# One product of 512 columns and one of 256 per weight block, a bank per output tile, and w_down behind w_up

## The chip, the cores and the metric

The kernel runs on one core of a Trainium2 chip. Times are device microseconds of one execution, from a profiler or from repeated timed runs; the number compared is the median of the timed runs. PE is the matrix engine, PEld its weight loads, DVE the vector engine, ACT the scalar engine, POOL the general engine, SP the engine whose queue issues the DMAs.

## The reference

Two blocks run one after the other on 256 positions of 1024 features. The change lies in the first block, in its output projection and its feed-forward part:

```python
x = x + jnp.einsum("bsd,de->bse", g_a * y_a + g_b * y_b, w_o[i])

h = rmsnorm(x, g_ffn[i])
u = jnp.einsum("bsd,df->bsf", h, w_up[i])                       # 1024 -> 2 * 2816
f_gate = causal_dwconv(u[..., :D_FF], conv_f_w[i]) + conv_f_b[i]   # 3 taps
f = jax.nn.gelu(f_gate, approximate=True) * u[..., D_FF:]
x = x + jnp.einsum("bsf,fd->bsd", f, w_down[i])                 # 2816 -> 1024

pg = jax.nn.sigmoid(jnp.einsum("bsd,de->bse", rmsnorm(x, g_ple[i]), w_ple_gate[i]))
x = x + pg * jnp.einsum("bsk,kd->bsd", p[i], w_ple[i])
...
```

Ahead of it stand a gated convolution mixer (w_in, w_a_out, w_b_out), behind it a final norm and a second block with windowed and differential attention and a feed-forward part of its own (w_up_2, w_down_2). All of it is float32.

## The kernel before

**Data.** Activations lie with features on the 128 partitions and the 256 positions along the free axis, so a tile of 128 features is 128x256. Weights come from memory in groups of eight blocks of 128x128 (`GROUPS`, 128x1024, 512 KB), in the order in which `_order` lists them; the names raw58, hi58 and lo58 carry the number of the group.

**Two parts.** Each float32 operand is split into a high part in the matrix engine's reduced format and the remainder. For a weight group, ACT casts raw into hi (`split_task`) and DVE subtracts to make lo; for an activation tile likewise, into two tiles called cr. A product of a weight block and an activation tile is three matrix products, which `run` issues: wh by xh, wh by xl, wl by xh, each of 256 columns, all three added up in one half of a PSUM bank (`Bank.half`). A bank (ps) holds two output tiles. Six hi and six lo buffers exist, and a split is begun four groups ahead of its use (`LEAD`).

**Order.** `Plan` is a small planner that runs when the program is built. It keeps a clock for every engine and writes each instruction into its engine's queue when the planner's clock says that its inputs are there; on the chip every queue runs in order, and waits are semaphores. Work around the products is written as generators (`f1_task`, `res_task`, `norm_task`) that the planner continues between matrix products (`plan.work`) or until a condition holds (`plan.until`).

**The stretch that is changed.** `w_o` has 8 x 8 weight blocks. When a pair of its output tiles is done, `res_task` adds x, makes the scaled split h2 of the new x, and squares it into a sum kept by POOL (`Sum`). `norm_task` takes the sum: a product with a column of 1/1024 (the tile is called mean in the profile and mean1024 in the program), an addition on DVE, a power of -0.5 on POOL (small), a product that spreads the two columns over the partitions (ident and small), and a copy by ACT into r2. `w_up` starts before r2 is there, on h2, which lacks that factor; `evac_pair` multiplies it in when a bank is taken out of PSUM. `w_up` has 22 pairs of tiles (gate j and value 22 + j), 16 blocks each. `f1_task` then does the convolution (one ACT instruction and two on DVE), the GELU, the product with the value tile and the split into `f[j]`. After pair j, `w_down` takes the eight blocks of row j - 4 (`LAG1`), adding to eight output tiles that keep four banks for the whole stretch. After the last row, `res_task` runs for all eight tiles, the sum and norm for r3 follow, and `w_ple_gate` goes on with h3.

Of the kernel before, what the change touches and what calls it, by code (L numbers as in the profile page):

```python
# [17 lines left out]
P = 128  # L18
# [25 lines left out]
LAG1, LAG2 = 4, 6  # L44
# [6 lines left out]
def _order():  # L51
# [17 lines left out]
    def ffn(up, down, n, lag, first, whole):  # L69
# [8 lines left out]
    ffn("w_up", "w_down", 22, LAG1, 2, False)  # L78
# [11 lines left out]
    ffn("w_up_2", "w_down_2", 32, LAG2, 4, True)  # L90
# [61 lines left out]

class Plan:
# [11 lines left out]
    def at(self, tiles):  # L165
        return max([self.written.get(t.tensor.name, 0.0) for t in tiles], default=0.0)

    def op(self, eng, cost, outs, ins, port=False):

        names = [t.tensor.name for t in outs]  # L170
# [15 lines left out]
        for t in ins:  # L186
            self.read[t.tensor.name] = max(self.read.get(t.tensor.name, 0.0), end)
# [133 lines left out]
def block_kernel(ctx: ExitStack, tc: tile.TileContext, w, xT, pT, vec, dist, gpost, out):  # L321
# [41 lines left out]
    NC = 79  # L363
# [4 lines left out]
    def cr():  # L368
        return ap.tile([P, T], F32R, tag="c", name=nm("cr"), bufs=NC)

    def pair():
        return ap.tile([P, 2, T], F32, tag="pair", name=nm("pair"), bufs=10)
# [76 lines left out]
    def run(key, dst, xs, lastk, hook=None):  # L449

        for n, b in enumerate(ORDER[key]):
# [6 lines left out]
            xh, xl = xs[k]  # L458
            plan.work(plan.at((wh, wl, xh, xl)))
# [5 lines left out]


    vt = cpool.tile([P, NV], F32, name="vt")
    gm = cpool.tile([P, 8], F32, name="gm")
    x = [cf() for _ in range(8)]
# [140 lines left out]
    def xn_task():  # L610
# [109 lines left out]
    def gate_task(c, q):  # L720
        yield [q.t]
        if c < 4:
            yield lambda: r1[0] is not None
            u = evac_pair(q, r1[0])
            yield [u]
        for i in range(2):
            g = cf()
            S.activation(g, u[:, i, :] if c < 4 else q.half(i), AF.Sigmoid, bias=vec1("b_gate", c + i))
            gates[c + i] = g
# [24 lines left out]
    def sc_task(c, q, qb):  # L754
# [12 lines left out]
        hi, lo = cr(), cr()  # L767
        S.copy(hi, qb.half(0))
        yield [hi]
        V.tensor_tensor(lo, qb.half(0), hi.bitcast(F32), op=ALU.subtract)  # L770
        shl[c] = hi, lo
# [37 lines left out]
    def yb_task(j, q):  # L809
        yield [q.t]  # L810
        for i in range(2):
            t = cf()
            V.tensor_tensor(t, q.half(i), gates[8 + j + i], op=ALU.mult)
            yb[j + i] = t
# [10 lines left out]
    def yp_task(j, q):  # L825
        yield [q.t]
        for i in range(2):
            t = cf()
            S.copy(t, q.half(i))
            yp[j + i] = t  # L830
# [17 lines left out]
    def mix_task(j, q):  # L848
        yield [q.t]
        for i in range(2):  # L850
            t = cf()
            V.tensor_tensor(t, q.half(i), gates[j + i], op=ALU.mult)
            V.tensor_tensor(t, t, yb[j + i], op=ALU.add)
            plan.spawn(split_task2(t, mix, j + i))
# [9 lines left out]
    def res_task(j, q, s, h, g):  # L864

        yield [q.t]
        for i in range(2):
            t = cf()
            V.tensor_tensor(t, q.half(i), x[j + i], op=ALU.add)
            x[j + i] = t  # L870
            hi = cr()
            S.activation(hi, t, AF.Identity, scale=vec1(g, j + i))
            plan.spawn(lo_scaled(t, hi, vec1(g, j + i), h, j + i, s))

    plan.spawn(norm_task(s2, DM, r2))
    qs = [Bank(), Bank()]
    run(("w_o", 0), {m: (qs[m // 2], m % 2) for m in range(4)}, mix, 7)
    plan.spawn(res_task(0, qs[0], s2, h2, "g_ffn"))
    plan.spawn(res_task(2, qs[1], s2, h2, "g_ffn"))
    del qs  # L880
    for j in (4, 6):
        q = Bank()
        run(("w_o", j), {j: (q, 0), j + 1: (q, 1)}, mix, 7)
        plan.spawn(res_task(j, q, s2, h2, "g_ffn"))
# [12 lines left out]
    def f1_task(j, q):  # L897
# [13 lines left out]
        V.tensor_tensor(c, c, u[:, 1, :], op=ALU.mult)  # L911
        ups[1] += 1
        yield [c]
        hi, lo = cr(), cr()
        S.copy(hi, c)
        yield [hi]
        V.tensor_tensor(lo, c, hi.bitcast(F32), op=ALU.subtract)
        f[j] = hi, lo

    ffn_first("w_up", 2, 22, h2, f1_task)  # L920
    down = [Bank() for _ in range(4)]
    ddst = {m: (down[m // 2], m % 2) for m in range(8)}
    for j in range(2, 22):
        plan.until(lambda: ups[0] > j - 4)
# [11 lines left out]
    for j in range(0, 8, 2):  # L936
        plan.spawn(res_task(j, down[j // 2], s3, h3, "g_ple"))
    del down, ddst
# [18 lines left out]
    def ple_task(j, q):  # L957
# [4 lines left out]
        ts = []  # L962
        for i in range(2):
            t = cf()
            S.activation(t, u[:, i, :], AF.Sigmoid)
            ts.append(t)
        if j == 6:
            preload(AF.Exp)
        hs = []
        for i in range(2):  # L970
# [5 lines left out]
            hi = cr()  # L976
            S.activation(hi, t, AF.Identity, scale=gfp[:, j + i : j + i + 1])
            hs.append(hi)
        for i in range(2):
            yield [hs[i]]  # L980
            lo = cr()
            V.scalar_tensor_tensor(
                lo, ts[i], gfp[:, j + i : j + i + 1], hs[i].bitcast(F32), op0=ALU.mult, op1=ALU.subtract
            )
            h4[j + i] = hs[i], lo
# [26 lines left out]
    def r45_task():  # L1012
# [23 lines left out]
        for j in range(8):  # L1036
            yield "dve"
            t = cf()
# [7 lines left out]
    def sc_tile(tag, bufs):  # L1046
        return ap.tile([P, 3 * P], F32, tag=tag, name=nm(tag), bufs=bufs)
# [86 lines left out]
    def swa_task():  # L1134
# [6 lines left out]
        for g in range(2):  # L1141
            pts = []
            for b in range(3):
# [4 lines left out]
                t = ap.tile([P, 512], F32, tag="pT", name=nm("pT"), bufs=4)  # L1148
# [16 lines left out]
        for b in range(2):  # L1165
            yield [yo[b].t]
            sq = ap.tile([P, 512], F32, tag="pT", name=nm("pT"), bufs=4)
# [17 lines left out]
        for c in range(4):  # L1185
# [7 lines left out]
            hi, lo = cr(), cr()  # L1193
            S.copy(hi, t)
            yield [hi]
            V.tensor_tensor(lo, t, hi.bitcast(F32), op=ALU.subtract)
            mix[c] = hi, lo
# [4 lines left out]
    for k in range(8):  # L1202
# [3 lines left out]
        plan.work(plan.at((wh, wl) + h4[k]))  # L1206
        for tt in range(2):
            plan.work()
            xh, xl = (z[:, tt * P : (tt + 1) * P] for z in h4[k])
# [38 lines left out]
    def diff_task(h, q):  # L1248
# [51 lines left out]
        hi, lo = cr(), cr()  # L1300
        S.copy(hi, y)
        yield [hi]
        V.tensor_tensor(lo, y, hi.bitcast(F32), op=ALU.subtract)
        mix[4 + h] = hi, lo
# [21 lines left out]
    for p in range(4):  # L1326
        sq = ap.tile([P, 512], F32, tag="pT", name=nm("pT"), bufs=4)
# [21 lines left out]
    def x5_task():  # L1349
        for j in range(8):  # L1350
            t = og[j // 2][:, j % 2, :]
            V.tensor_tensor(t, t, q6[:, T:], op=ALU.mult)
            n = cf()
            V.tensor_tensor(n, t, x[j], op=ALU.add)
            x[j] = n
            hi = cr()
# [183 lines left out]
```

## Time and profile before

| | before |
|---|---|
| median of 3 timed runs | 783.16 us (782.24 to 783.36) |
| the profiled execution's own time | 782.5 us |
| its span, first to last instruction | 780.7 us |
| PE busy | 762.9 us, 98% of the span |
| DVE busy | 613.3 us, 79% |
| ACT busy | 439.1 us, 56% |
| POOL busy | 95.1 us, 12% |
| granted PE clock, mean | 0.997 |

The span lies inside the execution's own time; 1.8 us are around it. Busy time of PE is modelled from pipelined products, so it tells that products are in flight, not that they could not follow each other faster. What a product costs is read from the distance between starts of neighbouring products.

### The profile page before, as it was taken

The page shows a single profiled execution, that of the slowest core. Times are in us where ns is not written, and L with a number is a line of the kernel's source. Part 1 is how long each engine was busy: PE and PEld are TensorE (multiplying, and loading weights), DVE is VectorE, ACT ScalarE, POOL GpSimd, SP SyncE. Part 2 cuts the span into 40 slices and gives each one's busy share as a digit, 9 for nine tenths or more (in the row PEclk, how much of TensorE's full clock was granted, in tenths as well). Part 3 has the DMA queues.
Part 4 walks back from the last instruction along what each step waited for, and adds up shares of the span by engine and source line. Part 5 has one row for each costly group of instructions (what it writes and reads, how often), then busy time and mean ns, then how long its engine had stood idle before and what let it go on. Part 6 is the DMA issues. An engine that isn't in the chain of part 4 may idle for free.

```text
span 780.7 us, 14974 instructions
## 1 busy us (share of the span) xinstructions
PE 762.9 (98%) x5892; PEld 735.2 (94%) x5892; DVE 613.3 (79%) x1099; ACT 439.1 (56%) x757; POOL 95.1 (12%) x75
## 2 busy tenths in 40 slices
PE   7999999999999999999999999999999999999996
PEld 6999999999999999999999799899999999999995
DVE  5699978877766676678679797789987877878783
ACT  6566465565544544456648655657755555554551
POOL 1589200040000000003200001220000000000000
PEclk9999999999999999999999999999999999999998
DMA  8757647564556555655344344363755555555631
GB/s 290 232 181 220 194 130 239 169 188 157 173 194 200 168 176 187 200 167 170 107 130 149 123 153 144 108 209 106 235 181 195 183 189 190 189 182 177 203 114 54
DMA packets 39670, 135.75 MB, mean 174 GB/s; under 512 B 4528, under 2 KB 6320, under 8 KB 39600
## 3 DMA queue, kind: packets, MB, share of 16 engines
q1 hardware_dynamic: 39600, 134.80, 53.5%
q8 instruction: 46, 0.75, 0.4%
q14 instruction: 24, 0.20, 0.1%
HBM read 133.73 MB, written 1.05 MB: 173 GB/s over the span
## 4 chain that ended last, share of the span: by engine, by line
PE 90%; DVE 3%; POOL 2%; issue 2%; DMA 1%; ACT 1%; SPq 0%; DVEq 0%; POOLq 0%
PE ps L272 90%; DVE cf L272 2%; POOL cf L272 2%; DVE lo L272 1%; DMA raw<-w_in 1%; DMA cf<-xT_in 1%; POOL small L272 0%; SPq L272 0%; ACT hi L272 0%; DVE pair L272 0%; ACT pT L272 0%; DVE cr L272 0%; DVEq L1535 0%; ACT cf L272 0%; DVE ps L272 0%
## 5 line engine op out<-in xcount | busy, mean ns | idle before, releaser
L272 PE MATMUL ps<-cr,hi 128*128 128x256 f32 x3408 | 621.8, 285 | 5.4 <-ACT hi L272 5.1
L272 PEld LDWEIGHTS ps<-cr,hi 128*128 128x128 f32 x3408 | 534.0, 192 | 10.0 <-ACT hi L272 5.5
L272 PE MATMUL ps<-cr,lo 128*128 128x256 f32 x1704 | 483.0, 283 | 0.8 <-DVE lo L272 0.8
L272 PEld LDWEIGHTS ps<-cr,lo 128*128 128x128 f32 x1704 | 327.3, 192 | 1.2 <-DVE lo L272 1.2
L272 DVE TENSOR_TENSOR lo<-raw,hi 128x1024 fp32r<-128x1024 f32 (+2 forms) x237 | 285.0, 1215 | 44.2 <-ACT hi L272 43.1
L272 ACT CAST hi<-raw 128x1024 fp32r<-128x1024 f32 (+2 forms) x255 | 258.7, 1027 | 45.9 <-PE ps L272 26.6
L272 ACT ACTIVATE cf<-pair,vt 128x256 f32<-128x256 f32 x90 | 50.0, 594 | 97.8 <-DVE pair L272 97.8
L272 DVE SCALAR_TENSOR_TENSOR cf<-pair,vt,cf 128x255 f32<-128x255 f32 (+1 forms) x172 | 80.1, 482 | 30.5 <-ACT cf L272 27.3
L272 PE MATMUL ps<-hi,cr 128*128 128x512 f32 (+2 forms) x320 | 98.2, 375 | 0.0
L272 PEld LDWEIGHTS ps<-hi,cr 128*128 128x128 f32 x320 | 58.9, 188 | 10.5 <-issue 1.0
L272 POOL TENSOR_TENSOR cf<-cf,cf 128x256 f32<-128x256 f32 x28 | 34.4, 1228 | 273.5 <-DVE cr L272 186.4
L272 POOL TENSOR_TENSOR small<-small,mh 128x2 f32<-128x2 f32 (+1 forms) x15 | 15.3, 1023 | 396.9 <-DVE small L272 396.9
L272 ACT CAST cr<-cf 128x256 fp32r<-128x256 f32 x76 | 30.5, 405 | 55.8 <-DVE cf L272 55.5
L272 PE MATMUL ps<-lo,cr 128*128 128x512 f32 (+2 forms) x160 | 60.0, 375 | 0.0
L272 ACT ACTIVATE cf<-cf 128x256 f32<-128x256 f32 x102 | 39.3, 411 | 33.7 <-DVE cf L272 33.7
L272 DVE TENSOR_TENSOR pair<-ps,cf 128x512 f32<-128x512 f32 x60 | 41.0, 688 | 16.7 <-PE ps L272 12.3
L272 DVE SCALAR_TENSOR_TENSOR cf<-ps,vt,cf 128x255 f32<-128x255 f32 (+30 forms) x136 | 51.9, 453 | 0.3 <-ACT cf L272 0.2
L272 POOL TENSOR_TENSOR lo<-raw,hi 128x1024 fp32r<-128x1024 f32 x18 | 42.9, 2419 | 10.0 <-ACT hi L272 10.0
L272 DVE TENSOR_TENSOR cr<-cf,cr 128x256 fp32r<-128x256 f32 x74 | 30.7, 421 | 11.8 <-ACT cr L272 11.7
L272 PEld LDWEIGHTS ps<-lo,cr 128*128 128x128 f32 x160 | 30.2, 189 | 4.0
L272 DVE TENSOR_TENSOR cf<-cf,cf 128x256 f32<-128x256 f32 x64 | 26.4, 420 | 1.0
L272 ACT ACTIVATE cr<-cf,vt 128x256 fp32r<-128x256 f32 x24 | 11.0, 502 | 16.6 <-DVE cf L272 16.5
(102 smaller groups left out, 302.4 us busy)
## 6 DMA issues: line engine op xcount, KB each, us to landing
raw<-w_in SPq DMA_DIRECT2D x244, 512.0 KB, 4.0
raw<-w_in SPq DMA_DIRECT2D x8, 320.0 KB, 2.9
cf<-xT_in SPq DMA_DIRECT2D x8, 128.0 KB, 5.7
out<-pT SPq DMA_DIRECT2D x3, 256.0 KB, 2.0
pair<-gpost_in SPq DMA_DIRECT2D x2, 256.0 KB, 5.9
vt<-vec_in SPq DMA_DIRECT2D x1, 420.5 KB, 5.9
dt<-dist_in SPq DMA_DIRECT2D x1, 384.0 KB, 5.8
raw<-w_in SPq DMA_DIRECT2D x2, 128.0 KB, 2.3
```

What stands on the lines that cost most here:

```text
L272: r = f(*args, **kw)
```

## The change

**Products.** `run2` takes the place of `run` for w_o, for w_up from pair 4 on, and for w_down. The two parts of an activation tile now stand side by side in one tile of 128x2x256 (`parts`), and the product of wh with both is one product of 512 columns into a whole bank; wl by xh follows with 256 columns into the bank's first half. The result is the sum of the two halves, so each output tile has a bank of its own, and the task that reads the bank adds the halves.

**Tasks.** `res2_task` adds x to the second half and then the first half to that, two DVE additions for one. `f1b_task` takes the place of `f1_task` from pair 4 on: ACT copies the second half of the gate's bank out, DVE adds it to the first half in PSUM, the convolution reads PSUM; the same for the value, whose product and split are done in PSUM. There the factor r2 can't be applied on the way out, since the banks hold unscaled halves; so `normed_task` makes a second, normalised split hn2 of x (one DVE multiplication, one ACT cast, one DVE subtraction per tile) for pairs 4 to 21. Pairs 0 to 3 (`OLD1`) go on as before.

**Order.** All of w_up comes first, then w_down, tile by tile over all 22 rows, the first two output tiles together (`DOWN1`).

**Buffers.** 79 buffers of 128x256 and 10 pairs become 16 and 56; gates, yb, yp and x move into pairs.

```diff
+    o["w_up", 0] = _blocks("w_up", (0, 22, 1, 23), r8)
+    for j in range(2, 22):
+        o["w_up", j] = _blocks("w_up", (j,), r8) + _blocks("w_up", (22 + j,), r8)
+    o["w_down", 0] = _blocks("w_down", range(DOWN1), range(22))
+    for m in range(DOWN1, 8):
+        o["w_down", m] = _blocks("w_down", (m,), range(22))
...
+    def run2(key, dst, xs, lastk):
+        for _, k, m in ORDER[key]:
+            if xs[k] is None:
+                plan.until(lambda: xs[k] is not None)
+            wh, wl = block((key[0], k, m))
+            xp = xs[k]
+            plan.work(plan.at((wh, wl, xp)))
+            q = dst[m]
+            mmul(q.t, wh, xp.rearrange("p a t -> p (a t)"), q.first(), False)
+            mmul(q.half(0), wl, xp[:, 0, :], False, k == lastk)
...
+    def f1b_task(j, qg, qv):
+        yield [qg.t]
+        t = cf()
+        S.copy(t, qg.half(1))
+        yield [t]
+        g = qg.half(0)
+        V.tensor_tensor(g, g, t, op=ALU.add)
+        yield [qg.t]
+        c = conv3_first(g, "conv_f_w", 22, j, "conv_f_b")
+        yield [c]
+        conv3_rest(c, g, "conv_f_w", 22, j)
+        ups[0] += 1
...
+        S.activation(c, c, AF.Gelu_apprx_tanh)
+        yield [qv.t]
+        t = cf()
+        S.copy(t, qv.half(1))
+        yield [t]
+        v = qv.half(0)
+        V.tensor_tensor(v, v, t, op=ALU.add)
+        yield [c, qv.t]
+        V.tensor_tensor(v, v, c, op=ALU.mult)
+        yield [qv.t]
+        hl = parts()
+        S.copy(hl[:, 0, :], v)
+        yield [hl]
+        V.tensor_tensor(hl[:, 1, :], v, hl[:, 0, :].bitcast(F32), op=ALU.subtract)
+        ups[1] += 1
+        f[j] = hl
...
     ffn_first("w_up", 2, 22, h2, f1_task)
-    for j in range(2, 22):
-        plan.until(lambda: ups[0] > j - 4)
+    for j in range(2, OLD1):
         q = Bank()
         run(("w_up", j), {j: (q, 0), 22 + j: (q, 1)}, h2, 7)
         plan.spawn(f1_task(j, q))
-        if j >= LAG1:
-            run(("w_down", j - LAG1), ddst, f, 21)
-    for k in range(22 - LAG1, 22):
-        run(("w_down", k), ddst, f, 21)
+    for j in range(OLD1, 22):
+        plan.until(lambda: ups[1] > j - 4)
...
+        qs = {j: Bank(), 22 + j: Bank()}
+        run2(("w_up", j), qs, hn2, 7)
+        plan.spawn(f1b_task(j, qs[j], qs[22 + j]))
```

**Where instructions stand.** On PE, in a w_up pair in the middle of the stretch (weights are hi and lo, ps is the bank, each pair of cr is one activation tile), the queue of before reads:

```order
L272 MATMUL ps294_3109<-cr209_2204,hi76_2969 128x256
L272 MATMUL ps294_3109<-cr216_2221,hi76_2969 128x256
L272 MATMUL ps294_3109<-cr209_2204,lo76_2971 128x256
L272 MATMUL ps294_3109<-cr211_2208,hi76_2969 128x256
L272 MATMUL ps294_3109<-cr217_2229,hi76_2969 128x256
L272 MATMUL ps294_3109<-cr211_2208,lo76_2971 128x256
```

and the changed one:

```order
L289 MATMUL ps260_2963<-cr202_2426,hi76_2846 128x512
L289 MATMUL ps260_2963<-cr202_2426,lo76_2862 128x256
L289 MATMUL ps260_2963<-cr207_2446,hi76_2846 128x512
L289 MATMUL ps260_2963<-cr207_2446,lo76_2862 128x256
```

Two weight blocks take four products where they took six; nothing else stands between them.

On DVE, in the middle of w_up, before (one pair of w_up with the w_down row behind it, three weight groups):

```order
L272 TENSOR_TENSOR lo105_3971<-raw105_3848,hi105_3969 128x1024
L272 TENSOR_TENSOR lo106_4001<-raw106_3870,hi106_3999 128x1024
L272 TENSOR_TENSOR pair337_4008<-ps334_3933,cf253_2505 128x512
L272 SCALAR_TENSOR_TENSOR cf338_4016<-pair337_4008,vt_69,cf338_4016 128x255
L272 SCALAR_TENSOR_TENSOR cf338_4016<-pair337_4008,vt_69,cf338_4016 128x254
L272 TENSOR_TENSOR cf338_4016<-cf338_4016,pair337_4008 128x256
L272 TENSOR_TENSOR lo107_4052<-raw107_3900,hi107_4037 128x1024
L272 TENSOR_TENSOR cr341_4047<-cf338_4016,cr340_4046 128x256
```

and now (one pair of w_up, two weight groups):

```order
L289 TENSOR_TENSOR ps243_2784<-ps243_2784,cf251_2848 128x256
L289 TENSOR_TENSOR cr252_2860<-ps237_2720,cr252_2860 128x256
L289 TENSOR_TENSOR lo77_2878<-raw77_2763,hi77_2876 128x1024
L289 SCALAR_TENSOR_TENSOR cf253_2882<-ps243_2784,vt_69,cf253_2882 128x255
L289 SCALAR_TENSOR_TENSOR cf253_2882<-ps243_2784,vt_69,cf253_2882 128x254
L289 TENSOR_TENSOR ps244_2785<-ps244_2785,cf254_2901 128x256
L289 TENSOR_TENSOR ps244_2785<-ps244_2785,cf253_2882 128x256
L289 TENSOR_TENSOR lo78_2923<-raw78_2797,hi78_2907 128x1024
```

Eight DVE instructions per pair stand in either order, but they now go with two weight groups and not with three, and the one of 512 columns has become two of 256.

On PE, where the norm for r2 stands in w_up's first pairs (w_up begins with group 56; mean1024 is the product of the sum, ident with small the one that spreads it), before:

```order
L272 MATMUL ps239_2376<-cr229_2306,lo58_2297 128x256
L272 MATMUL ps250_2475<-mean1024_99,cf249_2443 128x1 x2
L272 MATMUL ps238_2375<-cr231_2310,hi58_2295 128x256
...
L272 MATMUL ps239_2376<-cr231_2310,lo58_2297 128x256
L272 MATMUL ps250_2475<-ident_90,small252_2483 128x128 x2
L272 MATMUL ps238_2375<-cr241_2388,hi59_2335 128x256
```

and now:

```order
L289 MATMUL ps186_2261<-cr189_2268,lo59_2244 128x256
L289 MATMUL ps196_2388<-mean1024_95,cf195_2356 128x1 x2
L289 MATMUL ps186_2261<-cr189_2268,hi59_2238 128x256 x2
...
L289 MATMUL ps186_2261<-cr191_2280,lo59_2244 128x256
L289 MATMUL ps196_2388<-ident_86,small198_2396 128x128 x2
L289 MATMUL ps186_2261<-cr191_2280,hi59_2238 128x256 x2
```

The norm's first product has moved back by 21 products, from 60 behind the start of w_up to 81 behind it; the twelve products between it and the spreading one have stayed twelve.

## Rows read from the trace of the kernel before

**Rows 1.** The page: busy time (span's share), and the ending chain by engine.

```profile
PE 762.9 (98%) x5892; PEld 735.2 (94%) x5892; DVE 613.3 (79%) x1099; ACT 439.1 (56%) x757; POOL 95.1 (12%) x75
...
PE 90%; DVE 3%; POOL 2%; issue 2%; DMA 1%; ACT 1%; SPq 0%; DVEq 0%; POOLq 0%
```

**Rows 2.** Waits of PE, longest kind: us in total, times, longest.

```profile
PE ps L272 <- ACT hi L272: 5.1, 2, 4.5
```

**Rows 3.** Windows: busy us of each engine in w_up and w_down.

```profile
193.00:345.00 152.00, 152.00 (x1269) 152.00 (x1268) 107.76 (x145) 77.15 (x109) 0.00 (x0) 1.00 0.56 184
```

**Rows 4.** Timeline of PE in w_up: start us, us, instruction, count.

```profile
329.95 0.40 PE L272 MATMUL ps<-cr,hi 128*128 128x256 f32 x2
...
331.75 0.40 PE L272 MATMUL ps<-cr,hi 128*128 128x256 f32 x2
```

**Rows 5.** Timeline of PE, twelve products of 512 columns in w_down_2.

```profile
610.61 0.40 PE L272 MATMUL ps<-hi,cr 128*128 128x512 f32 x1
...
611.77 0.62 PE L272 MATMUL ps<-hi,cr 128*128 128x512 f32 x2
...
613.36 0.40 PE L272 MATMUL ps<-cr,hi 128*128 128x256 f32 x2
613.59 0.28 PE L272 MATMUL ps<-cr,lo 128*128 128x256 f32 x1
```

**Rows 6.** Groups of DVE by shape, 176 to 375 us: busy us, mean ns, idle before.

```profile
L272 DVE TENSOR_TENSOR lo<-raw,hi 128x1024 fp32r<-128x1024 f32 x68 | 83.9, 1235 | 17.6 <-ACT hi L272 16.9
L272 DVE TENSOR_TENSOR pair<-ps,cf 128x512 f32<-128x512 f32 x22 | 15.1, 690 | 12.3 <-PE ps L272 12.3
...
L272 DVE SCALAR_TENSOR_TENSOR cf<-pair,vt,cf 128x255 f32<-128x255 f32 x22 | 10.6, 483 | 11.7 <-ACT cf L272 11.6
L272 DVE TENSOR_TENSOR cf<-cf,pair 128x256 f32<-128x256 f32 x22 | 9.3, 425 | 10.2 <-ACT cf L272 10.2
```

**Rows 7.** Groups of DVE by shape, 0 to 180 us.

```profile
L272 DVE TENSOR_TENSOR ps<-ps,cf 128x256 f32<-128x256 f32 x16 | 6.5, 426 | 0.3
...
L272 DVE TENSOR_TENSOR cr<-ps,cr 128x256 fp32r<-128x256 f32 x12 | 5.0, 419 | 0.9 <-ACT cr L272 0.9
```

**Rows 8.** Groups of ACT by shape, 0 to 180 us.

```profile
L272 ACT CAST hi<-raw 128x1024 fp32r<-128x1024 f32 x62 | 64.5, 1046 | 28.2 <-DMA raw<-w_in 13.0 <-PE ps L272 12.8 <-issue 1.7
L272 ACT ACTIVATE cf<-ps,vt 128x256 f32<-128x256 f32 x20 | 8.9, 488 | 11.2 <-DVE ps L272 8.9 <-PE ps L272 2.2
L272 ACT ACTIVATE cf<-cf 128x256 f32<-128x256 f32 x24 | 8.3, 409 | 2.9 <-DVE cf L272 2.9
...
L272 ACT COPY cf<-ps 128x256 f32<-128x256 f32 x14 | 4.8, 377 | 6.9 <-PE ps L272 6.9
```

**Rows 9.** Timeline of DVE in a stretch where its queue is never empty.

```profile
83.51 1.22 DVE L272 TENSOR_TENSOR lo<-raw,hi 128x1024 fp32r<-128x1024 f32 x1
84.64 1.55 DVE L272 SCALAR_TENSOR_TENSOR cf<-ps,vt,cf 128x230 f32<-128x230 f32 x4
...
90.19 0.43 DVE L272 TENSOR_TENSOR ps<-ps,cf 128x256 f32<-128x256 f32 x1
90.52 0.81 DVE L272 SCALAR_TENSOR_TENSOR cf<-ps,vt,cf 128x228 f32<-128x228 f32 x2
```

**Rows 10.** Timeline of PE, the norm for r2 in w_up.

```profile
175.76 0.50 PE L272 MATMUL ps<-mean,cf 128*128 128x1 f32 x4
...
178.22 0.71 PE L272 MATMUL ps<-ident,small 128*128 128x128 f32 x4 [0.42 <-POOL small L272]
```

**Rows 11.** Timeline of ACT, the copy of r2.

```profile
178.97 0.38 ACT L272 COPY cf<-ps 128x256 f32<-128x256 f32 x1 [3.47 <-PE ps L272]
```

**Rows 12.** Timeline of POOL behind w_down: the sum for r3.

```profile
364.60 10.03 POOL L272 TENSOR_TENSOR cf<-cf,cf 128x256 f32<-128x256 f32 x7 [186.43 <-DVE cr L272]
```

**Rows 13.** Timeline of PE, the norm for r3 in w_ple_gate.

```profile
373.39 0.28 PE L272 MATMUL ps<-cr,lo 128*128 128x256 f32 x1
374.68 0.61 PE L272 MATMUL ps<-mean,cf 128*128 128x1 f32 x4 [1.01 <-POOL cf L272]
```

More of the change, by code (lines that the diff above doesn't have):

```diff
@@ L150, with _cells @@
 ACT_SETS = (AF.Sigmoid, AF.Silu, AF.Gelu_apprx_tanh, AF.Exp)
+def _cells(t):
+    name, shape = t.tensor.name, t.tensor.shape
+    if len(shape) != 3 or shape[1] != 2 or shape[2] != T:
+        return [name]
+    lo = t.offset % (2 * T)
+    hi = lo + sum((c - 1) * s for s, c in t.ap[1:])
+    return [(name, i) for i in range(lo // T, hi // T + 1)]
 class Plan:
@@ L186, in op @@
         for t in ins:
-            self.read[t.tensor.name] = max(self.read.get(t.tensor.name, 0.0), end)
+            for n in _cells(t):
+                self.read[n] = max(self.read.get(n, 0.0), end)
         if eng == "pe":
@@ L826, in yp_task @@
         yield [q.t]
+        t = pair()
+        S.copy(t, q.pair())
         for i in range(2):
-            t = cf()
-            S.copy(t, q.half(i))
-            yp[j + i] = t
+            yp[j + i] = t[:, i, :]
     for j in range(0, 8, 2):
@@ L935, in block_kernel @@
     plan.spawn(norm_task(s3, DM, r3))
-    for j in range(0, 8, 2):
-        plan.spawn(res_task(j, down[j // 2], s3, h3, "g_ple"))
-    del down, ddst
+    xnew = [None] * 4
+    qs = [Bank() for _ in range(DOWN1)]
+    run2(("w_down", 0), qs, f, 21)
+    for j in range(DOWN1):
+        plan.spawn(res2_task(j, qs[j], s3, h3, "g_ple"))
+    del qs
+    for j in range(DOWN1, 8):
+        q = Bank()
+        run2(("w_down", j), {j: q}, f, 21)
+        plan.spawn(res2_task(j, q, s3, h3, "g_ple"))
+        del q
     nsink = small(8, "nsink", 1)
@@ L1046, in sc_tile @@
     def sc_tile(tag, bufs):
-        return ap.tile([P, 3 * P], F32, tag=tag, name=nm(tag), bufs=bufs)
+        return ap.tile([P, 3 * P], F32, tag="pair", name=nm(tag), bufs=NPAIR)
     live = [0]
@@ L1326, in block_kernel @@
     for p in range(4):
-        sq = ap.tile([P, 512], F32, tag="pT", name=nm("pT"), bufs=4)
+        sq = ap.tile([P, 512], F32, tag="pair", name=nm("pT"), bufs=NPAIR)
         S.activation(sq, ob[p].t, AF.Square)
@@ L1407, in block_kernel, with run_half @@
     down = [[Bank() for _ in range(2)] for _ in range(2)]
-    def run_half(tt, k, wh, wl, fh, fl, banks=(0, 1)):
-        plan.work(plan.at((wh, wl, fh, fl)))
-        a, b = (z[:, tt * P : (tt + 1) * P] for z in (fh, fl))
+    def run_half(tt, k, wh, wl, fp, banks=(0, 1)):
+        plan.work(plan.at((wh, wl, fp)))
+        a, b = (fp[:, i, tt * P : (tt + 1) * P] for i in range(2))
         for i in banks:
@@ L1421, in run_down @@
             plan.until(lambda: f[k] is not None)
-        ops = block(ORDER["w_down_2", k][0], 8) + f[k]
+        ops = block(ORDER["w_down_2", k][0], 8) + (f[k],)
         f[k] = ()
@@ L1476, in block_kernel @@
             plan.until(lambda: f[k] is not None)
-        ws.append(block(ORDER["w_down_2", k][0], 8) + f[k])
+        ws.append(block(ORDER["w_down_2", k][0], 8) + (f[k],))
     for tt in range(2):
```

247 lines of the change are left out of this document (148 added, 99 removed).

## Prediction

> **What bounds the kernel now.** I read the page first. PE is busy for 762.9 of 780.7 us and 90% of the chain that ended last lies on it [rows 1]; no other engine comes near. PE's busy time is modelled, though, so I asked next what PE waits for: the longest kind is 5.1 us in two waits in the whole kernel [rows 2], and in 152 us of w_up and w_down PE is busy without a gap at granted clock 1.00 [rows 3]. In that stretch DVE is busy for 107.76 of 152 us, ACT for 77.15, POOL not at all. So the stretch takes as long as its products take to follow each other, and any gain must come from there. Any loss must come from DVE or ACT being late, and they have room at present.
>
> What a product costs is the distance between starts. From 329.95 to 331.75 stand 15 products of 256 columns [rows 4]: 1.80 / 15 = 0.120 us. In w_down_2 stand twelve of 512 columns, each with weights of its own, from 610.61 to 613.36 [rows 5]. Five start from 610.61 to 611.77, 0.232 us each; seven from 611.77 to 613.36, 0.227 us each. Twice 0.120 is 0.240: the wide product is cheaper than two narrow ones by 0.013 us, at worst by 0.008.
>
> **The products.** w_o has 64 weight blocks, the 18 pairs of w_up from pair 4 on have 16 each, w_down has 22 x 8: 64 + 288 + 176 = 528 blocks. Each loses one product and one weight load, and keeps its 768 columns. A block took 3 x 0.120 = 0.360 us and will take 0.227 + 0.120 = 0.347. That saves 528 x 0.013 = 6.9 us (w_o 0.8, w_up 3.8, w_down 2.3). Bounds: with 0.232 it is 528 x 0.008 = 4.2 us. On the other side, the two narrow products behind the last wide one start at 613.36 and the next at 613.59 [rows 5], 0.115 each. If a narrow one beside a wide one costs that, a block takes 0.342 and 528 x 0.018 = 9.5 us are saved. I take 6.9: it uses the longer series at both widths, and in the changed order each wide product follows a narrow one, for which the trace has only single cases.
>
> The Trainium skill, page "TensorE: Matmul & The Clock Gate", section "Back-to-back issue gap", gives N/2.4 + 2.5 ns between starts at the full clock, which would be 109 and 216 ns here. The rows show 120 and 227, so the trace does not agree: 11 ns more at either width. By the page one product saved would be worth 2.5 ns, an estimate of 1.3 us over 528 blocks where the rows give 6.9.
>
> **DVE and ACT in w_up.** A w_up pair now takes PE 16 x 0.347 = 5.55 us. In this time DVE has two weight splits of 1.235 [rows 6], three operations in PSUM of 0.426, one subtraction of 0.419 [rows 7] and two convolution taps of 0.483 [rows 6]: 2.47 + 1.28 + 0.42 + 0.97 = 5.14 us of durations. Durations overlap in a full queue: a weight split is followed after 1.13 us, an operation of 256 columns after 0.33, and four taps take 1.55 together, so one start follows the last by (1.55 - 0.44) / 3 = 0.37 [rows 9]. By starts: 2 x 1.13 + 4 x 0.33 + 2 x 0.37 = 4.3 us, 78% of 5.55. ACT has two casts of 1.046, two copies of 0.377, the convolution's first tap 0.488, the GELU 0.409 [rows 8], and a cast from PSUM that I price as a copy: 4.1 us, 74%. Both fit, so I cost all added work of f1b_task at nothing; what hides it is PE's 5.55 us, and the margin is 0.4 us by durations and 1.2 by starts. A pair has two of the eight banks and its task holds them for some three weight groups in the queue's order, while their next user starts six groups after the pair's end. In w_down DVE has one weight split per 2.8 us and two additions of 0.42 per 7.6 us: nothing waits. DMAs stay one of 512 KB per weight group, and a group's PE time falls by 4% only, from 2.88 to 2.78 us, so SP's queue has the same work.
>
> **The normalised copies.** This is the place where the change adds a wait. Pair 4 needs hn2, and its PE products stand at the head of an in-order queue, so everything behind them waits as well. Counted from the start of w_up: the norm's first product stands behind 81 products and not 60, so at 9.7 us and not 7.2. From it to the end of r2's copy are 178.97 + 0.38 - 175.76 = 3.6 us [rows 10, 11], so r2 is there at 13.3. From there to the last hn2 the DVE queue has 27 instructions: twelve of scalar and tensor, ten of 256 columns, three bank evacuations of 0.690 [rows 6], two weight splits. By starts that is 12 x 0.37 + 10 x 0.33 + 3 x 0.69 + 2 x 1.13 = 12.1 us, by durations 12 x 0.48 + 10 x 0.42 + 2.07 + 2.47 = 14.5. The last copy is ready at 25.4 to 27.8. PE comes to pair 4 after 192 products, 23.0 us, plus the norm's own: 178.22 - 175.76 and some 0.5 for the spreading step make 3.0, with twelve products of 1.44 in it, so 1.5. That is 24.5, and it asks for the eighth tile seven blocks later, at 24.5 + 7 x 0.347 = 26.9. Margin: +1.5 us by starts, -0.9 by durations. The queue is full here, so I take starts and cost it at nothing; the bound is some 1 us, up to 3 if ACT's casts between add their waits.
>
> **The norms.** For r2 the twelve products between the norm's two steps stay, and so does PE's wait of about 0.6 us at 178.22 (2.46 from the first step less 1.44 and the step's own 0.4) [rows 10]: no difference. Behind w_down, PE waits 1.01 us for POOL [rows 13], since POOL adds seven squares in 10.03 us [rows 12] after all eight tiles end together. In the new order the tiles end 7.6 us apart and one addition is left: two DVE additions (0.8), ACT's scaled cast and square (0.9), one addition by POOL (10.03 / 7 = 1.4), handoffs 0.2: 3.3 us behind w_down's end, where the norm's first step stands 24 products or 2.9 us behind it. Wait 0.4. The spreading step follows after 15 products, 1.8 us, and needs 2.46 - 0.4: wait 0.3. So 0.7 in place of 1.0: 0.3 us gained. The attention part has the same work in a slightly different order, with two groups of transposes drawn together; I give it 0, within 1 us either way.
>
> **Sum.** 6.9 + 0.3 = 7.2 us off the profiled execution's 782.5, so 775.3. That execution lies 0.7 below the median of the runs shown, 783.2; on the median the sum gives 776.0.
>
> **Rivals.**
> - *The wide product saves more* (block 0.342): 9.5 + 0.3 us, 773.4. For it, the 0.115 [rows 5]; against it, it is one pair of starts in two decimals.
> - *hn2 or the first f1b tasks late*: the copies by durations, then a DVE queue that starts the new pairs with a debt. PE loses 1 to 3 us at pair 4 and perhaps as much again before the debt is worked off: 777.5 to 781.5.
> - *The change doesn't do what it says*: the alternation of widths makes each wide product cost the full 0.240, toward the 0.232 seen right behind narrow ones [rows 5]. Then nothing is saved but 0.3: 783. Against it, seven wide products at 0.227. The Trainium skill's rule above would end near here too, at 781.9.
> - *Slower*: DVE sets the pace of w_up. Today's queue waits 11.6 us for ACT ahead of 22 first taps and 10.2 ahead of 22 GELU products [rows 6], 0.99 us a pair. If these waits stay with durations of 5.14, a pair takes 6.13 us on DVE and not 5.55 on PE: 18 x 0.58 = 10.4 us, 776.0 + 10.4 = 786.4. It decides above (7.2 + 1.6) / 18 = 0.49 us a pair, or a period of 6.04. For it, the new task has two more crossings from ACT to DVE. Against it, the waits come from a queue with idle time, weight splits of other groups stand between the steps of one pair, and splits begin four groups, 11 us, ahead, which would have to be used up first.
>
> **How the numbers follow.** A measurement of this kernel can tell 0.2%, 1.6 us, from no change. Products as priced, with bounds of 4.2 saved and 1 us from the attention part: 0.62 for 774.5 to 779. More saved: 0.10, 772.5 to 774.5. Late copies: 0.15, 779 to 781.5. Nothing saved: 0.05. Slower: 0.08. The likeliest gives 776.0. A range from 773.0 to 780.8 leaves out the last two cases, and the edges of the second and third. Faster: 0.62 + 0.10 + 0.14 = 0.86; same: 0.06; slower: 0.08.
>
> **What would show it.** Right: wide to narrow 0.227 and narrow to wide 0.120 in PE's timeline of w_down; PE without gaps from pair 4 of w_up to the end of w_down; DVE near 80% in w_up and far below in w_down. Wrong: PE waiting for cr (hn2) at pair 4, for DVE lo in w_up, or for ps; a block of 0.36; a stretch of the attention part that is longer by over 1 us.

## The result

The changed kernel takes 777.44 us (median of 4, 776.84 to 777.74); the kernel before, timed on the same chip, takes 782.7 (781.5 to 783.36). The ratio is 0.9934 [0.9916, 0.9951], which is 5.3 us faster where 7.2 were predicted. 777.44 lies 1.4 us above the predicted 776.0 and inside the range; the likeliest case is the one that came, with a smaller gain. The gain is 1.9 us short; 0.5 of that doesn't show in the time, since the kernel before took 782.7 here and 783.2 in the runs that the prediction started from.

The page of the changed kernel: span, busy time and share of each engine, and the chain that ended last, by engine.

```profile
span 775.5 us, 14017 instructions
...
PE 758.4 (98%) x5364; PEld 706.2 (91%) x5364; DVE 628.7 (81%) x1149; ACT 451.9 (58%) x797; POOL 90.8 (12%) x75
...
PE 83%; DVE 10%; issue 2%; POOL 1%; DMA 1%; ACT 1%; SPq 1%; POOLq 0%; DVEq 0%; ACTq 0%
```

528 PE instructions and as many weight loads are gone (5892 less 5364) [rows 1], one for each of the 528 blocks, as counted. PE is still 98% busy; DVE's share of the chain has grown from 3 to 10%.

The same view as [rows 3], now of most of w_up from pair 4 on and most of w_down (bounds in us, busy us of PE, PEld, DVE, ACT and POOL with their counts, granted clock, DMA share, GB/s):

```profile
198.00:292.00 94.00, 94.00 (x533) 81.56 (x533) 83.36 (x143) 63.48 (x120) 0.00 (x0) 1.00 0.62 198
296.00:354.00 58.00, 58.00 (x331) 50.29 (x330) 37.13 (x49) 27.18 (x39) 6.20 (x6) 1.00 0.54 181
```

PE has no gap in either, at granted clock 1.00. DVE is busy for 83.36 of 94 us in w_up, 89%, and for 64% in w_down. So the stretch is still as long as its products take to follow each other, and the first thing to read is their distance. PE's timeline in the middle of w_up (start us, us, instruction, count):

```profile
250.10 0.40 PE L289 MATMUL ps<-cr,hi 128*128 128x512 f32 x1
250.34 0.28 PE L289 MATMUL ps<-cr,lo 128*128 128x256 f32 x1
250.46 0.40 PE L289 MATMUL ps<-cr,hi 128*128 128x512 f32 x1
250.70 0.28 PE L289 MATMUL ps<-cr,lo 128*128 128x256 f32 x1
250.81 0.40 PE L289 MATMUL ps<-cr,hi 128*128 128x512 f32 x1
251.04 0.28 PE L289 MATMUL ps<-cr,lo 128*128 128x256 f32 x1
251.16 0.40 PE L289 MATMUL ps<-cr,hi 128*128 128x512 f32 x1
```

Three blocks take 251.16 - 250.10 = 1.06 us, 0.353 each. From wide to narrow are 0.24, 0.24 and 0.23 us, from narrow to wide 0.12, 0.11 and 0.12. Over all of 200 to 290 us (some 255 distances of each kind) the means are 236.7 and 116.7 ns, together 353.4. The prediction had 227 + 120 = 347.

Where the 5.2 us between the two profiled executions (spans 780.7 and 775.5) lie, by the starts of PE's first product of each stage:

| stretch | before | after | difference |
|---|---|---|---|
| up to w_o | 145.52 | 145.30 | -0.22 |
| w_o | 23.04 | 22.61 | -0.43 |
| w_up, pairs 0 to 3 | 24.59 | 24.59 | 0.00 |
| w_up from pair 4, and w_down | 167.04 | 163.95 | -3.09 |
| w_ple_gate and the stage behind it | 41.95 | 40.74 | -1.21 |
| the rest of the attention part | | | -0.37 |
| second feed-forward part | | | +0.1 |

w_o and the long stretch hold all 528 blocks: 3.52 us, or 528 x 6.6 ns (360 - 353.4) = 3.5. The 1.21 us of the next part lie around the norm behind w_down. POOL in the changed kernel, three additions of the sum and the power:

```profile
343.93 1.41 POOL L289 TENSOR_TENSOR cf<-cf,cf 128x256 f32<-128x256 f32 x1 [6.35 <-issue]
350.76 0.73 POOL L289 TENSOR_TENSOR cf<-cf,cf 128x256 f32<-128x256 f32 x1 [5.42 <-ACT cf L289]
358.54 0.74 POOL L289 TENSOR_TENSOR cf<-cf,cf 128x256 f32<-128x256 f32 x1 [7.05 <-ACT cf L289]
360.75 0.70 POOL L289 TENSOR_TENSOR small<-small,mh 128x2 f32<-128x2 f32 x1 [1.47 <-DVE small L289]
```

and PE at the norm's two steps behind w_down, and at the spreading step of the norm after it:

```profile
359.22 0.28 PE L289 MATMUL ps<-cr,lo 128*128 128x256 f32 x1
359.33 0.60 PE L289 MATMUL ps<-mean,cf 128*128 128x1 f32 x4
...
361.56 0.28 PE L289 MATMUL ps<-cr,lo 128*128 128x256 f32 x1
361.68 0.60 PE L289 MATMUL ps<-ident,small 128*128 128x128 f32 x4
...
389.62 0.28 PE L289 MATMUL ps<-cr,lo 128*128 128x256 f32 x1
390.46 0.60 PE L289 MATMUL ps<-ident,small 128*128 128x128 f32 x3 [0.57 <-DVE small L289]
```

Neither step behind w_down has a bracket: the wait of 1.01 us [rows 13] is gone altogether, 1.17 by starts (374.68 - 373.39, less the product's own 0.12). At 390.46 stands one of 0.72 by starts (0.84 less 0.12). The kernel before loses 0.19 at the same step (0.31 less 0.12):

```profile
396.89 0.28 PE L272 MATMUL ps<-cr,lo 128*128 128x256 f32 x1
397.20 0.71 PE L272 MATMUL ps<-ident,small 128*128 128x128 f32 x4
```

So 0.53 us are new, and 1.21 - 1.17 + 0.53 = 0.57 us are left. Most of that lies in the 32 products of 2 columns called gsq, which both kernels have: from the start of each to the start of the next product they take 3.62 us before and 3.14 now, in groups of other sizes. PE's waits, us in total, times, longest:

```profile
PE ps L289 <- ACT hi L289: 4.4, 2, 4.2
...
PE ps L289 <- POOL cf L289: 1.8, 2, 1.0
...
PE ps L289 <- DVE small L289: 0.6, 1, 0.6
...
PE ps L289 <- DVE cr L289: 0.3, 1, 0.3
```

No wait for hn2 is in it: the 0.3 for cr stands at 493.28, in the attention part. hn2's last split is the last of these three on DVE:

```profile
192.77 1.09 DVE L289 TENSOR_TENSOR cr<-cf,cr 128x256 fp32r<-128x256 f32 x3
```

It ends at 193.86. Pair 4 starts at 192.51 and asks for the eighth tile 7 x 0.353 later, at 194.98. The margin is 1.1 us.

### The profile page after: what moved, and what is told of

The parts are those of the page before. It is cut to its first block, busy times and chain, and to the rows that moved or that the text cites. A ratio compares the mean times of both kernels' runs of the same rounds, so it can differ in the third digit from the quotient of the medians.

```text
span 775.5 us, 14017 instructions
## 1 busy us (share of the span) xinstructions
PE 758.4 (98%) x5364; PEld 706.2 (91%) x5364; DVE 628.7 (81%) x1149; ACT 451.9 (58%) x797; POOL 90.8 (12%) x75
## 4 chain that ended last, share of the span: by engine, by line
PE 83%; DVE 10%; issue 2%; POOL 1%; DMA 1%; ACT 1%; SPq 1%; POOLq 0%; DVEq 0%; ACTq 0%
PE ps L289 83%; DVE cf L289 7%; DVE lo L289 1%; POOL cf L289 1%; DMA pair<-xT_in 1%; DVE ps L289 1%; SPq L289 1%; POOL small L289 1%; DVE pair L289 0%; DVE cr L289 0%; ACT cf L289 0%; DMA raw<-w_in 0%; ACT hi L289 0%; ACT pT L289 0%; ACT cr L289 0%
## 5 line engine op out<-in xcount | busy, mean ns | idle before, releaser
L289 PE MATMUL ps<-cr,hi 128*128 128x256 f32 (+1 forms) x2880 | 618.2, 306 | 4.8 <-ACT hi L289 4.4
L289 PEld LDWEIGHTS ps<-cr,hi 128*128 128x128 f32 x2880 | 468.0, 191 | 34.4 <-ACT hi L289 4.6
L289 DVE SCALAR_TENSOR_TENSOR cf<-pair,vt,cf 128x254 f32<-128x254 f32 (+2 forms) x144 | 66.5, 482 | 19.8 <-ACT cf L289 17.3
L289 DVE SCALAR_TENSOR_TENSOR cf<-ps,vt,cf 128x255 f32<-128x255 f32 (+30 forms) x172 | 69.2, 460 | 5.4 <-ACT cf L289 4.6
L289 ACT ACTIVATE cf<-pair,vt 128x256 f32<-128x256 f32 x68 | 37.5, 599 | 49.6 <-DVE pair L289 49.6
L289 ACT ACTIVATE cf<-cf 128x256 f32<-128x256 f32 x62 | 25.3, 417 | 23.9 <-DVE cf L289 23.9
L289 DVE TENSOR_TENSOR pair<-ps,cf 128x512 f32<-128x512 f32 (+1 forms) x58 | 35.6, 616 | 3.1 <-ACT cf L289 1.9
L289 DVE TENSOR_TENSOR cr<-cf,cr 128x256 fp32r<-128x256 f32 x64 | 26.3, 421 | 11.8 <-ACT cr L289 11.7
L289 ACT ACTIVATE cr<-pair,vt 128x256 fp32r<-128x256 f32 x24 | 12.2, 510 | 40.2 <-DVE pair L289 40.1
L289 DVE TENSOR_TENSOR ps<-ps,cf 128x256 f32<-128x256 f32 x70 | 29.6, 428 | 3.3 <-ACT cf L289 2.4
```

The lines of the kernel that those rows point to most:

```text
L289: r = f(*args, **kw)
```

## The experiments

Each is an edit of the changed kernel, timed against the kernel before on the same chip. The first question is why a block costs 353 and not 347 ns.

**e1_narrow: the new order with the old products.** The wide product becomes two narrow ones again; tasks, order and buffers stay.

```diff
-            mmul(q.t, wh, xp.rearrange("p a t -> p (a t)"), q.first(), False)
+            mmul(q.half(0), wh, xp[:, 0, :], q.first(), False)
+            mmul(q.half(1), wh, xp[:, 1, :], False, False)
             mmul(q.half(0), wl, xp[:, 0, :], False, k == lastk)
```

> The changed kernel with its order, banks, tasks and norms, but each wide product split again into two of 256 columns into the same bank: three products per block. Theory 'products': the changed trace shows 353.4 ns per block and the narrow form 360, so 528 blocks bring 3.5 of the 5.2 us, and this kernel comes to 780.9 us, with 1.7 us left that the order and the norm behind w_down bring. Rival 'order': all 5.2 us come from fewer waits, and this kernel stays at 777.4. Rival 'products alone': the order brings nothing, and it comes to 782.7.

Measured: 781.21 us (11 runs) against 782.0, ratio 0.9990 [0.9981, 0.9999]; span 779.0. All distances in w_up are 120.0 ns. By the spans the products are worth 779.0 - 775.5 = 3.5 us, the sum that the distances gave, and the rest 780.7 - 779.0 = 1.7. By the timed medians (ratios 0.9990 and 0.9934 of 782) it is 4.4 and 0.8. The interval of the first (2.8 to 5.9) holds 3.5; that of the second (0.1 to 1.5) ends just short of 1.7. The stages decide: by starts of PE, e1_narrow takes 23.04 us for w_o and 167.04 from pair 4 to the end of w_down, both to 0.01 us what the kernel before takes; 1.6 of its 1.7 us lie behind w_down. The products bring most of the gain, and the new order and the longer tasks cost nothing in the stretch that holds them.

**e2_batch8 and e3_batch2: the widths in longer turns.** The narrow products are held back until eight, or two, wide ones have gone. Each product keeps its weights and bank.

```diff
-        for _, k, m in ORDER[key]:
+        held = []
+        for n, (_, k, m) in enumerate(ORDER[key]):
...
-            mmul(q.half(0), wl, xp[:, 0, :], False, k == lastk)
+            held.append((q, wl, xp, k))
+            if len(held) == 2 or pos[1] == 0 or n == len(ORDER[key]) - 1:
+                for q, wl, xp, k in held:
+                    mmul(q.half(0), wl, xp[:, 0, :], False, k == lastk)
+                held = []
```

Eight:

> The changed kernel, with the same products in another order: within a weight group all eight wide products first, then the eight narrow ones. Theory 'turns': a wide product costs 233 to 241 ns only near a change of width, and 227 in a series, as in w_down_2. Then a group takes about 8 x 0.230 + 8 x 0.119 = 2.79 us and not 2.83, and 66 groups give 2.3 us: 775.1. Rival 'place': a wide product costs 236 here whatever stands beside it (its moving operand is an activation pair, its bank takes both halves): 777.4, no change.

Measured: 781.05 us (11 runs) against 782.0, ratio 0.9987 [0.9978, 0.9996]. The distances came as expected: from 208 to 290 us, at granted clock 1.00, a group of eight blocks takes 2.79 us, 349.2 ns a block, so the rival 'place' is out. The time missed all the same. PE waited for hn2 at pair 4 (timeline of PE, as above):

```profile
193.57 0.50 PE L289 MATMUL ps<-cr,hi 128*128 128x512 f32 x1 [0.17 <-DVE cr L289]
194.84 0.50 PE L289 MATMUL ps<-cr,hi 128*128 128x512 f32 x1 [0.77 <-DVE cr L289]
197.22 0.80 PE L289 MATMUL ps<-cr,hi 128*128 128x512 f32 x1 [1.89 <-DVE cr L289]
```

The pair starts at 191.78, and eight wide products in a row ask for the eighth tile 7 x 0.233 later, at 193.4; with turns of one it was 194.98. And the tile comes later: DVE's row for it is

```profile
196.75 0.42 DVE L289 TENSOR_TENSOR cr<-cf,cr 128x256 fp32r<-128x256 f32 x1
```

which ends at 197.17, 0.05 ahead of PE's start, where it was 193.86: the planner, whose times the turns change, wrote one more weight split and a pair's two taps into DVE's queue ahead of it, and r2 itself came 0.7 us later. So 1.6 us sooner and 3.3 later against a margin of 1.1: the rival of the late copies, come true. The waits for cr add up to 3.0 us in four. Then the clock fell, as the windows show (columns as above; the granted clock is the third from the end):

```profile
192.00:198.00 6.00, 3.15 (x9) 1.62 (x8) 5.96 (x13) 5.48 (x11) 0.00 (x0) 0.85 0.41 132
198.00:201.00 3.00, 3.00 (x13) 2.71 (x12) 2.96 (x7) 1.63 (x4) 0.00 (x0) 0.50 0.68 249
201.00:204.00 3.00, 3.00 (x15) 2.52 (x14) 2.83 (x6) 1.81 (x4) 0.00 (x0) 0.67 0.49 176
204.00:207.00 3.00, 3.00 (x19) 2.62 (x19) 2.10 (x3) 1.71 (x4) 0.00 (x0) 1.00 0.76 209
```

PE was busy for 3.15 of 6 us; from 198 on it is busy without a gap, but at 0.50, the 1.2 GHz level, and it is back at 2.4 GHz only by 204. From pair 4 to the end of w_down this kernel takes 168.6 us and not 163.95. By starts, the eighth wide product comes 3.8 us late (197.22 for 193.4); from it to the third group, at 203.94, PE takes 6.7 us for what takes 4.0 at granted clock 1.00; the cheaper blocks give 1.9 back.

Two:

> As the run before, with turns of two: two wide products, then two narrow ones. Theory 'turns': half as many changes of width, so half of the gap to 347 ns per block is won: 350 ns, 528 x 3.3 = 1.8 us, 775.6. Rival 'place': 777.4.

Measured: **774.37 us** (773.56 to 774.67, 4 runs) against 782.0, ratio 0.9904 [0.9891, 0.9918]; span 772.5, 3.0 less than the changed kernel. PE's timeline:

```profile
249.79 0.62 PE L289 MATMUL ps<-cr,hi 128*128 128x512 f32 x2
250.25 0.40 PE L289 MATMUL ps<-cr,lo 128*128 128x256 f32 x2
250.48 0.63 PE L289 MATMUL ps<-cr,hi 128*128 128x512 f32 x2
...
251.88 0.63 PE L289 MATMUL ps<-cr,hi 128*128 128x512 f32 x2
```

Six blocks in 251.88 - 249.79 = 2.09 us are 0.348 each. 528 x (353.4 - 348.3) ns = 2.7 us, nearly the whole difference of the spans: the distance is the gain. It is more than the expected 350 ns. Of the 5 ns a block that are won, 3.5 lie in the wide product.

**e8_batch4: turns of four.** The same edit with 4.

> The changed kernel with turns of four wide and four narrow products. From the places in a series that the turns of eight showed (wide 233.3, 235.5, 232.1, 235.5; narrow 114.6, 119.0, 119.9, 119.8) a block takes 234.1 + 118.3 = 352.4 ns, where turns of two took 348.3 and turns of one 353.4. Theory 'narrow behind wide': what is won is the narrow product right behind a wide one, so four turns are worth 528 x 1.0 ns = 0.5 us against the changed kernel, 776.9, and turns of two stay best. Rival 'fewer turns are better': under 774.4.

Measured: 775.91 us (4 runs) against 783.11 on another chip, ratio 0.9913 [0.9898, 0.9928], not to be told from turns of two by the timed runs. The distances tell them apart: 350.8 ns a block, and turns of two stay best. The expected 352.4 rests on places in the turns of eight that the trace does not give: at granted clock 1.00 the first four are 233.3, 235.7, 228.3 and 232.7 for wide products and 113.3, 119.3, 120.0 and 120.0 for narrow ones, which make 350.6. The theory 'narrow behind wide' is not borne out, since turns of two win most in the wide product.

**e4_384 and e5_wide: the narrow product made wider.** These ask why the wide product costs 237. Either its weights, loaded under a narrow product, come late; or a change of width costs; or these tiles and banks make wide products dear. In both, wl is multiplied with part or all of the second half too, which adds work and a term that the reference has not.

```diff
-            mmul(q.t, wh, xp.rearrange("p a t -> p (a t)"), q.first(), False)
-            mmul(q.half(0), wl, xp[:, 0, :], False, k == lastk)
+            xw = xp.rearrange("p a t -> p (a t)")
+            mmul(q.t, wh, xw, q.first(), False)
+            mmul(q[:, :384], wl, xw[:, :384], False, k == lastk)
```

(e5_wide has `mmul(q.t, wl, xw, False, k == lastk)` in the last line.)

> The changed kernel with the narrow product widened to 384 columns (it also adds the product of the two low parts for the first 128 positions, which the reference rounds away). One look, for the distances between starts alone. Theory 'load': what is lost at a turn is the weight load of the wide product, which begins when the narrow one starts and isn't done after 0.113 us; behind 384 columns (0.175 us) it is done, and the wide product costs 227. Theory 'turn of width': any change of width costs, and it stays at 233 to 241. Rival 'place' gives 236 too. Time about 777.4 + 528 x 0.05 = 804 us.

> The changed kernel with both products of a block 512 columns wide (the second also adds the product of the two low parts, which the reference rounds away). One look, for the distances between starts. The turns of eight showed the first wide products of a series at 233 to 236 ns and the last ones mostly at 227. Theory 'series': an endless series of wide ones settles at 227, 0.454 per block, 777.4 + 528 x 0.101 = 831 us. Rival 'place': wide products on this data cost 233 to 237 for good, 0.470 per block, 839 us.

Measured, one run each: 809.04 and 830.82 us. PE's timeline of e4_384, and its weight load for the last of these products:

```profile
250.09 0.40 PE L289 MATMUL ps<-cr,hi 128*128 128x512 f32 x1
250.33 0.34 PE L289 MATMUL ps<-cr,lo 128*128 128x384 f32 x1
250.50 0.40 PE L289 MATMUL ps<-cr,hi 128*128 128x512 f32 x1
...
250.33 0.19 PEld L289 LDWEIGHTS ps<-cr,hi 128*128 128x128 f32 x1
```

and of e5_wide:

```profile
250.00 0.39 PE L289 MATMUL ps<-cr,hi 128*128 128x512 f32 x1
250.23 0.39 PE L289 MATMUL ps<-cr,lo 128*128 128x512 f32 x1
```

With 176 ns between the 384-column product and the next one, where the narrow one left 117, the wide product still costs 237.3 ns on the mean. By the trace its load takes 0.19 us, so here it is late by 14 ns and not by 73; a cost that grows with the lateness falls. That any lateness costs 10 ns falls by e3_batch2: there the load of the second wide product starts with the first one, 0.23 us ahead of its own product, which costs 233.5 all the same. With one width throughout, on the same tiles and banks, every one of 397 distances from 200 to 290 us is 226 or 227 ns: tiles and banks fall. What is left is that wide products cost more where widths change.

**e6_dve2 and e7_dve4: how near is DVE to setting the pace?** DVE is 89% busy in w_up, by durations of which some overlap. Two or four idle multiplications are added per pair of w_up; their result is not used.

```diff
         f[j] = hl
+        for _ in range(2):
+            V.tensor_tensor(c, c, c, op=ALU.mult)
```

> The changed kernel with two more DVE multiplications of 256 columns at the end of each of the 18 f1b tasks, whose results nobody reads. A pair then has 5.14 + 0.84 = 5.98 us of DVE durations and 4.3 + 0.66 = 5.0 us by starts, against 5.65 us of PE. Theory 'starts': DVE keeps up, 777.4. Rival 'durations': DVE falls behind by 0.33 us a pair, 5.9 us over 18 pairs, less what the splits' lead covers: up to 783.

> As the run before, with four more multiplications: 5.14 + 1.68 = 6.8 us of durations a pair, 4.3 + 1.32 = 5.6 by starts, against 5.65 of PE. Theory 'starts': just at the edge; 777.4 to 780, PE begins to wait for lo or for banks at the end of w_up. Rival 'durations': 18 x 1.17 = 21 us, less the lead of some 11: 787 or more.

Measured: 778.58 and 787.79 us against 783.11 (4 runs each); ratios 0.9948 [0.9933, 0.9963], which overlaps that of the changed kernel, and 1.0062 [1.0045, 1.0079]. From pair 4 to the end of w_down e6_dve2 takes 163.95 us, to 0.01 us what the changed kernel takes; the 1.5 us by which its span is longer lie behind w_down, 0.8 of them at 435.52, where PE waits for POOL, and most of the rest between 470 and 500 us, where the granted clock is 0.94 and the changed kernel has 1.00. e7_dve4 takes 173.92 for the stretch. Windows of w_up of e6_dve2:

```profile
198.00:245.00 47.00, 47.00 (x268) 40.77 (x267) 46.19 (x87) 31.13 (x60) 0.00 (x0) 1.00 0.66 204
```

of e7_dve4, in w_up and across the start of w_down:

```profile
198.00:245.00 47.00, 47.00 (x268) 40.77 (x267) 46.10 (x89) 30.34 (x56) 0.00 (x0) 1.00 0.63 194
...
306.00:320.00 14.00, 7.96 (x34) 6.09 (x34) 13.19 (x28) 3.92 (x7) 0.00 (x0) 0.79 0.61 197
```

and PE's timeline of e7_dve4 there:

```profile
312.73 0.50 PE L289 MATMUL ps<-cr,hi 128*128 128x512 f32 x1 [2.54 <-DVE cr L289]
...
316.79 0.80 PE L289 MATMUL ps<-cr,hi 128*128 128x512 f32 x1 [3.09 <-DVE cr L289]
```

Both keep DVE at 98% in w_up, and PE has no gap there in either. One is on schedule, the other late, and the busy share does not tell which. The debt of e7_dve4 comes due in w_down, when its first two tiles reach the last rows: four waits for the last splits of f, 6.3 us in total, with the clock at 0.79 over the 14 us around them. Starts alone had expected 780 at most, durations 787 or more; the idle operations hang on each other and start 0.45 us apart, where a queue of independent ones pays 0.33. With that price a pair takes DVE some 5.1 us by starts in e6_dve2 and 6.0 in e7_dve4, an estimate from the prediction's 4.3, where PE takes 5.65. The reserve in w_up lies between two and four such operations a pair.

## Why the prediction was right, and which term was off

The time came within 1.4 us partly by luck: the products gave 3.4 us less than their term, and the places that were priced at 0.3 gave 1.7.

**The products (predicted 6.9 us, at least 4.2; measured 3.5).** This is the mis-sized term, and it lies below its own lower bound. The step that failed is "I take 6.9: it uses the longer series at both widths". The series were read rightly: e1_narrow has 120.0 throughout, e5_wide 226.7 throughout. But the changed order is no series: a wide product between narrow ones costs 236.7, above even the 232 of [rows 5] that the prediction took as its worst, and a narrow one behind a wide one 116.7, near the 115 of its best. The rival of the dearer wide product saw one half of this and the rival of the cheaper narrow one the other; together they leave half the gain. The pair 232 and 115 of [rows 5], five distances and two, would have given 347 as well; only the two in turn show 353. That trace had more than single cases, though: w_down_2 has 25 such turns of twelve, and the wide product behind a narrow one takes 233.6 ns in them and the next 235.9. The 0.115 was a reading in two decimals: the first narrow product behind a wide one takes 113 ns, the second 119.4.

**The norm behind w_down (predicted 0.3; measured 1.2 with the stage behind it).** The wait went, and none of the predicted 0.7 came in its place. POOL's addition took 0.74 us and its power 0.70, where the addition was priced at 10.03 / 7 = 1.4, a mean of unlike ones (see the last section). But 0.72 us are lost at 390.46 where the kernel before lost 0.19, and the prediction did not have this wait. Won and lost make 0.64 us, twice the 0.3; of the other 0.57, 0.48 are the shorter time of the products called gsq, which the prediction had not priced either, and why they are shorter stays open.

**The norm in w_up (predicted no difference).** The spreading step starts at 180.09, 0.70 us behind the narrow product ahead of it, so the wait is 0.58, the predicted 0.6.

**The normalised copies (predicted +1.5 us by starts, -0.9 by durations).** Ready 25.95 us after the start of w_up, where 25.4 was predicted by starts and 27.8 by durations; margin +1.1. The choice of starts was right in a full queue. e2_batch8 shows what the place costs when the margin is used up.

**DVE in w_up (predicted near 80%).** 89%, so 5.0 us a pair: near the 5.14 of durations in what is shown as busy, while PE never waited. The rival of DVE setting the pace needed more than two further operations a pair; its loss then fell in w_down and not in w_up. Waits of DVE for ACT did not stay as they were, as that rival assumed: the 94 us of w_up shown above have 9.2 us of them, of all kinds, so 0.55 a pair and not 0.99.

**The attention part** gave -0.37 us, within the 1 us allowed.

## What to carry to other kernels

Price a product from the distance in the very order that the change makes, not from series of each width; if widths alternate, two and two are worth trying before anything else (774.37 us against 777.44 here, where the kernel before took 782.0 and 782.7 beside them). When a faster engine asks earlier for what another one makes, work out the margin in us at the place where it is asked for: 1.1 us held here, and where a reordering of products used it up, waits and then a slow clock took more than the reordering gave. For an engine at 98% look where its work is due, since neither its busy share nor a gap at that place tells whether it is late.

## What the runs showed of the hardware

Distances between starts of products with weights of their own, float32 in the reduced format, at granted clock 1.00:

| order | wide product (512) | product between | per block |
|---|---|---|---|
| 256 only (e1_narrow) | | 120.0 | 360.0 (three) |
| 512 only (e5_wide) | 226.7 | | |
| 512 and 384 in turn (e4_384) | 237.3 | 176.0 | 413.3 |
| 512 and 256 in turn (changed kernel) | 236.7 | 116.7 | 353.4 |
| two and two (e3_batch2) | 232.9 and 233.5 | 114.5 and 115.8 | 348.3 |
| four and four (e8_batch4) | 234.2, 234.5, 232.1, 228.4 | 117.5, 119.7, 118.7, 118.3 | 350.8 |
| eight and eight (e2_batch8, from 208 us) | 233.3, 235.7, 228.3, 232.7, 230.6, then 226.7 | 113.3, 119.3, then 120.0 | 349.2 |
| twelve 512 between 256 (kernel before, w_down_2) | 233.6, 235.9, 228.1, 232.4, 230.6, then 226.7 | 113.0, 119.4, then 120.0 | |

Behind a change of width five wide products are 1 to 9 ns dearer than in their series, and from the sixth on they cost what they cost there; the first narrow one is 7 ns cheaper, and from the third on narrow ones cost 120. The two long orders show the same places on other weights, tiles and banks. Short turns can't be added up from these places: the first ones make 346.6 ns for turns of one and the first two 350.8 for turns of two, where 353.4 and 348.3 were measured. Why is open: weight loads, tiles and banks are ruled out by e4_384, e3_batch2 and e5_wide, and nothing was measured that shows what is left.

The Trainium skill, page "TensorE: Matmul & The Clock Gate", section "Back-to-back issue gap", gives one gap per width, N/2.4 + 2.5 ns, for an isolated product at the full clock, and says itself that weight loads change it in a stream. That is 109 ns at 256 columns and 216 at 512, estimates from the page; the runs show 120.0 and 226.7 in series and 113 to 120 and 227 to 237 in turns, so the trace does not agree, and it shows that the gap depends on the neighbour's width too.

POOL's additions above are the same instruction at 1.41, 0.73 and 0.74 us. DVE's timeline of the changed kernel around the first two:

```profile
343.51 4.08 DVE L289 TENSOR_TENSOR lo<-raw,hi 128x1024 fp32r<-128x1024 f32 x3 [0.45 <-ACT hi L289]
...
350.34 0.48 DVE L289 SCALAR_TENSOR_TENSOR cr<-pair,vt,cr 128x256 fp32r<-128x256 f32 x1 [0.58 <-ACT cr L289]
351.59 2.36 DVE L289 TENSOR_TENSOR lo<-raw,hi 128x1024 fp32r<-128x1024 f32 x2 [0.76 <-ACT hi L289]
```

During the addition of 1.41 DVE splits weights; during that of 0.73 it stands idle but for the first 0.06 us. The seven additions of [rows 12] are not alike either: the first four take 1.60 to 2.48 us, the last three 2.34 together (POOL, then DVE):

```profile
372.28 2.34 POOL L272 TENSOR_TENSOR cf<-cf,cf 128x256 f32<-128x256 f32 x3
...
370.04 1.56 DVE L272 TENSOR_TENSOR lo<-raw,hi 128x1024 fp32r<-128x1024 f32 x1
375.32 0.16 DVE L272 TENSOR_SCALAR small<-ps 128x2 f32<-128x2 f32 x1 [3.71 <-PE ps L272]
```

DVE stands idle during those three. It is not DVE's work as such: at 501.45 in the changed kernel the addition takes 0.74 us with DVE busy throughout, and DVE's own instruction, which starts 0.05 us behind it, takes 0.97 where its like at 350.34 took 0.48:

```profile
501.45 0.74 POOL L289 TENSOR_TENSOR cf<-cf,cf 128x256 f32<-128x256 f32 x1 [2.07 <-ACT cf L289]
...
501.50 0.97 DVE L289 SCALAR_TENSOR_TENSOR cr<-pair,vt,cr 128x256 fp32r<-128x256 f32 x1
```

Every addition over 1.1 us in the changed kernel lies beside a weight split of DVE, but a few beside a split take 0.74 to 0.80, so what decides is not shown, and an edit that takes DVE's work away alone was not run.
